# One transformer layer on one core: wider weight blocks in the second part of the first feed-forward input, and a new spread of the adaptive-norm rows

## The chip, the core and the metric

The kernel runs on one core of one Trainium2 chip, in one launch. The metric is the device time of the execution in microseconds. The time before is the median of 3 runs.

## What is computed

One layer with two feed-forward blocks around a token mixer. Every block is preceded by a modulated layer norm and followed by a gated residual and a second layer norm. The nine vectors of shift, scale and gate come from one condition vector `c`, through a matrix `w_ada` of 2048 x 18432:

```
ada = (jax.nn.silu(c) @ w_ada + b_ada)[:, None, :]
sh1, sc1, g1, sh2, sc2, g2, sh3, sc3, g3 = jnp.split(ada, N_ADA, axis=-1)
h = _swiglu(_modulate(x, sh1, sc1), ffn1_w_in, ffn1_w_out)
x = _layernorm(ALPHA * x + 0.5 * (1 + g1) * h, ln1_g, ln1_b)
h = _token_mixer(_modulate(x, sh2, sc2), w_in, ..., w_out)
x = _layernorm(ALPHA * x + (1 + g2) * h, ln2_g, ln2_b)
h = _swiglu(_modulate(x, sh3, sc3), ffn2_w_in, ffn2_w_out)
x = _layernorm(ALPHA * x + 0.5 * (1 + g3) * h, ln3_g, ln3_b)
```

`_swiglu` is `(silu(gate) * up) @ w_out`, where `gate` and `up` are the two halves of `h @ w_in`. There are 256 tokens, the model width is 2048, the feed-forward width 5632. All data is 32-bit floating point. The token mixer holds eight attention heads with a forget gate and four mLSTM heads.

## The kernel before

**Products.** Each weight block of 1 MB is loaded from memory by the SyncE queue (SP) into one of three `raw` buffers, and split into a high part (cast on ScalarE, line 155) and a low part (subtraction on VectorE, line 156), in two halves of 128 x 1024 elements. There are six buffers for each part, three blocks' worth. TensorE multiplies in three passes, high x high, high x low, low x high (`mm3`, lines 420 to 422).

**Stages, in order.** (1) The first four condition units and the first part of the first feed-forward input, `first_in`, names `s`: weight blocks of 512 inputs x 512 columns. (2) The second part of that input, `ffn_in`, names `f1i`: column pairs 12 to 21 of 256 columns each, gate and up. One step is one block of 1024 inputs x 256 columns. (3) The first output projection, `out_proj` with tag `f1`, names `f1o`: column groups of 1024, 512 and 512; a step ("unit") is 1 MB, so there are 22, 11 and 11 of them. The products of the last four units are kept for the end, where a layer norm (`boundary`) follows without a pause. (4) The mixer, steps of 1 MB each: output gate (`mo`), values (`fv`, `mv`), mLSTM queries and keys (`m`), attention queries and keys (`fb`, `fbk`, `fa`, `fak`), its output projection (`mxo`). `form_a_four` there takes its weights in blocks of 512 inputs x 512 columns. Between the products run the heads' short chains, written as generators that each step advances. (5) A second boundary, and the second feed-forward block (`gu`, `fh`, `fs`, `f2i`, `f2o`).

**The ada rows.** The product with `w_ada` is not done on TensorE. A unit of 1024 columns is built from 16 rows of 128 x 1024 elements. A row is one load of 512 KB (`ar`, line 189, on SP) into one of two `araw` buffers, and one multiply-add of 128 x 1024 on VectorE into an accumulator (`ada_acc`, lines 168 and 170). After the 16th row a tail of five small steps sums over the partitions (split, a TensorE product `bc`, and more VectorE work, lines 176 to 217).

**What sets their order.** `AdaQueue` holds 14 such units. After each weight step the program calls `pump(rate)`: the rate is added to what is owed, one tail step is made if a tail is open, and whole rows that are owed are issued. Each row is put behind the newest low part (`pinned`). A unit that uses the common accumulator can't begin while the tail of another such unit is open; what is owed meanwhile is issued afterwards. Units carry a stage number: seven may start in stage 0, four more after the first boundary, three after the second. `need(n)` finishes n units at once, where their result is used: 2 units before the first output projection, 6 at the first boundary, 10 late in the mixer's projection, then 11, 12 and 14. The rates (line 797) are `R_F` 1.25 in the end of the first part, `R_IN` 1.2 in `f1i`, `R_OUT` 1 in `f1o`, `R_MX` 1.42 in the mixer, `R_A` 1.05 and `R_B` 0.6 in the second block. In the last column group of an output projection the last four units issue no rows.

A step's loads, casts and multiply-adds run ahead of TensorE by what the buffers allow. VectorE takes its instructions in the order in which they were placed: a multiply-add whose row hasn't landed holds up what stands behind it.

The column loop of the second part, before, with its two cases; the first feed-forward takes the first of them:

```
for j in range(j0, DFF // 256):
    if values is None:
        ps = [mm_tile(f"gu_{tag}{j}_{f}") for f in range(2)]
        for gu in range(2):
            one(j, gu, [p[:, gu * T:(gu + 1) * T] for p in ps])
```

Of the kernel before, what the change touches and what calls it, by code (L numbers as in the profile page):

```python
# [14 lines left out]
P = 128  # L15
# [17 lines left out]
def layer_kernel(  # L33
# [408 lines left out]

    def ffn_in(w, xT, hT, j0, tag, npump, values=None):
        def one(j, gu, outs):
            last = gu and j == DFF // 256 - 1
            cols_form_a(w, gu * DFF + j * 256, outs, xT, f"{tag}i{j}_{gu}", (lambda: None) if last else npump)

        def both(dst, ps):
# [3 lines left out]
        for j in range(j0, DFF // 256):  # L452
            if values is None:
                ps = [mm_tile(f"gu_{tag}{j}_{f}") for f in range(2)]
                for gu in range(2):
                    one(j, gu, [p[:, gu * T:(gu + 1) * T] for p in ps])
                for f in range(2):
                    h = halves(hT[:, 2 * j + f, :])
                    S.activation(h, unwoven(ps[f][:, :T]), AF.Silu)
                    pin["h"] = V.tensor_tensor(out=h, in0=h, in1=unwoven(ps[f][:, T:]), op=ALU.mult).ins  # L460
                continue
            for gu in range(2):
                ps = [mm_tile(f"gu_{tag}{j}_{gu}{f}") for f in range(2)]
                one(j, gu, ps)
                for f in range(2):
                    h = halves(hT[:, 2 * j + f, :])
                    if gu:
                        u = halves(values.tile([P, T], F32, tag="u", bufs=2, name=f"u_{tag}{j}_{f}"))
                        both(u, ps[f])
                        pin["h"] = V.tensor_tensor(out=h, in0=h, in1=u, op=ALU.mult).ins  # L470
                    else:
                        both(h, ps[f])
                        S.activation(h, h, AF.Silu)
        for _ in range(2):
            npump()
# [3 lines left out]
    def out_proj(w, rows, nk, tag, npump, finish, before=None, turned=False, spare=None, fine=None):  # L479
# [12 lines left out]
        for width in (1024, 512, 512):  # L492
# [56 lines left out]
            for i, u in enumerate(us):  # L549
# [246 lines left out]

    R_F, R_IN, R_OUT, R_MX, R_A, R_B = 1.25, 1.2, 1, 1.42, 1.05, .6
    NP = 2
# [258 lines left out]
    first_hi_places("1")  # L1057
    ffn_in(W1, xT, hT, NS, "f1", at(R_IN))
    xp.release()
# [658 lines left out]
```

## Time and profile before

| what | value |
|---|---|
| median of 3 runs | 1876.1 us (1875.28 to 1876.51) |
| profiled execution, its own time | 1878.46 us |
| span of its trace | 1876.8 us |
| TensorE busy | 1829.0 us, 97% of the span |
| VectorE busy | 1465.0 us, 78% |
| ScalarE busy | 911.8 us, 49% |
| memory traffic | 510.74 MB, mean 272 GB/s |
| ada row loads | 230 on SP and 45 on GpSimd, 512 KB each |

PE is TensorE's multiplying, PEld its loading of weights, DVE is VectorE, ACT ScalarE, POOL GpSimd, SP SyncE. A row of a group reads: line, engine, operation, output and inputs with shapes, count, busy time in us and mean in ns, then idle time just before and what ended it. In rows by stretch of time, "DMA share" is the mean busy share of the 16 DMA engines, which can come out a little over 1, and PEclk is the clock that TensorE was granted.

### The profile page before, as it was taken

What the parts mean: (1) busy time and instruction counts of PE and PEld (TensorE: products, weight loads), DVE (VectorE), ACT (ScalarE), POOL (GpSimd) and SP (SyncE); (2) the same over time, 40 slices, a digit from 0 to 9 for tenths busy, and PEclk for the clock granted to TensorE, in tenths of its full rate; (3) what the DMA queues carried; (4) which work ended last, traced back from release to release, by engine and by line L of the source; (5) the groups of instructions that cost most, each with busy time, mean ns of one, the idle gap of its engine ahead of it and who ended that gap; (6) DMA issues with size and microseconds to landing.
All of it is one profiled execution on the core that took longest, in us unless ns stands there. A gap on an engine that the chain in (4) does not pass through costs nothing.

```text
span 1876.8 us, 29775 instructions
## 1 busy us (share of the span) xinstructions
PE 1829.0 (97%) x11881; PEld 1673.8 (89%) x11881; DVE 1465.0 (78%) x1883; ACT 911.8 (49%) x1320; POOL 62.2 (3%) x92
## 2 busy tenths in 40 slices
PE   7999999999999999999989999999999999999997
PEld 5999999999998888699989887888999999988887
DVE  6888989778788886878879788988977766574655
ACT  3554363443454433845556545565444454554441
POOL 1211200000000000100000000000000000000000
PEclk9999999999999999999999999999999999999999
DMA  9988978999998898489978894998878776666664
GB/s 365 383 279 294 333 232 274 313 312 325 296 315 305 309 329 296 136 301 331 316 254 307 303 314 142 307 305 265 271 253 265 260 241 193 201 202 204 205 204 146
DMA packets 283906, 510.74 MB, mean 272 GB/s; under 512 B 10834, under 2 KB 134386, under 8 KB 282744
## 3 DMA queue, kind: packets, MB, share of 16 engines
q1 hardware_dynamic: 275656, 477.90, 75.0%
q0 software_dynamic: 8112, 30.95, 4.8%
q8 instruction: 93, 1.52, 0.3%
q14 instruction: 45, 0.37, 0.1%
HBM read 506.71 MB, written 2.10 MB: 271 GB/s over the span
## 4 chain that ended last, share of the span: by engine, by line
PE 38%; DMA 10%; DVE 8%; issue 2%; ACT 2%; POOL 0%; DVEq 0%; ACTq 0%; SPq 0%; POOLq 0%
PE gu_f L425 9%; DMA ar<-in_w_ada_dram 7%; PE gu_f L426 4%; PE o_f L421 4%; PE o_f L420 4%; PE o_f L422 4%; PE fs L425 3%; DMA raw_fh<-in_ffn_w_in_dram 2%; DVE acc L170 2%; PE fs L426 1%; DVE gate L170 1%; PE fh L425 1%; PE b_mv L421 1%; PE b_mv L420 1%; PE b_mv L422 1%
## 5 line engine op out<-in xcount | busy, mean ns | idle before, releaser
L170 DVE SCALAR_TENSOR_TENSOR acc<-ar,csil,acc 128x1024 f32<-128x1024 f32 (+1 forms) x167 | 211.7, 1269 | 74.3 <-DMA ar<-in_w_ada_dram 73.7
L425 PE MATMUL gu_f<-x_f,hi_f2i 128*128 128x512 f32 x768 | 251.8, 382 | 0.0
L422 PE MATMUL s<-x_f,lo_s 128*128 128x256 f32 x768 | 211.9, 276 | 0.8 <-DVE lo_s L156 0.7
L420 PE MATMUL s<-x_f,hi_s 128*128 128x256 f32 x768 | 212.2, 277 | 0.2 <-ACT x_f L336 0.2
L421 PE MATMUL s<-x_f,hi_s 128*128 128x256 f32 x768 | 212.0, 276 | 0.0
L426 PE MATMUL gu_f<-x_f,lo_f2i 128*128 128x256 f32 x768 | 209.3, 273 | 0.0
L422 PE MATMUL gu_f<-x_f,lo_f1i 128*128 128x256 f32 x640 | 176.4, 276 | 1.4 <-DVE lo_f1i L156 1.3
L421 PE MATMUL gu_f<-x_f,hi_f1i 128*128 128x256 f32 x640 | 176.0, 275 | 0.0
L420 PE MATMUL gu_f<-x_f,hi_f1i 128*128 128x256 f32 x640 | 176.0, 275 | 0.0
L156 DVE TENSOR_TENSOR lo_f2o<-raw_f2o,hi_f2o 128x1024 fp32r<-128x1024 f32 x86 | 105.2, 1225 | 86.9 <-ACT hi_f2o L155 86.8
L156 DVE TENSOR_TENSOR lo_f2i<-raw_f2i,hi_f2i 128x1024 fp32r<-128x1024 f32 x96 | 117.5, 1224 | 65.7 <-ACT hi_f2i L155 64.8
L425 PEld LDWEIGHTS gu_f<-x_f,hi_f2i 128*128 128x128 f32 x768 | 145.1, 189 | 20.3
L155 ACT CAST hi_s<-raw_s 128x1024 fp32r<-128x1024 f32 x96 | 99.5, 1051 | 128.7 <-PE s L421 77.0
L422 PEld LDWEIGHTS s<-x_f,lo_s 128*128 128x128 f32 x768 | 147.9, 193 | 1.2 <-DVE lo_s L156 1.2
L421 PEld LDWEIGHTS s<-x_f,hi_s 128*128 128x128 f32 x768 | 147.9, 193 | 0.4 <-DVE x_f L339 0.4
L420 PEld LDWEIGHTS s<-x_f,hi_s 128*128 128x128 f32 x768 | 147.8, 193 | 0.3 <-ACT x_f L336 0.3
L426 PEld LDWEIGHTS gu_f<-x_f,lo_f2i 128*128 128x128 f32 x768 | 147.4, 192 | 0.2
L155 ACT CAST hi_f2o<-raw_f2o 128x1024 fp32r<-128x1024 f32 x86 | 90.0, 1047 | 115.7 <-PE o_f L422 107.5
L155 ACT CAST hi_f2i<-raw_f2i 128x1024 fp32r<-128x1024 f32 x96 | 100.4, 1045 | 91.3 <-PE gu_f L425 65.3
L155 ACT CAST hi_f1o<-raw_f1o 128x1024 fp32r<-128x1024 f32 x86 | 88.5, 1047 | 113.7 <-DMA raw_f1o<-in_ffn_w_out_dram 55.0
L170 DVE SCALAR_TENSOR_TENSOR gate<-ar,csil,gate 128x1024 f32<-128x1024 f32 (+1 forms) x94 | 117.6, 1252 | 29.0 <-DMA ar<-in_w_ada_dram 28.9
L155 ACT CAST hi_f1i<-raw_f1i 128x1024 fp32r<-128x1024 f32 x80 | 81.3, 1049 | 111.6 <-DMA raw_f1i<-in_ffn_w_in_dram 80.2
(449 smaller groups left out, 5095.4 us busy)
## 6 DMA issues: line engine op xcount, KB each, us to landing
ar<-in_w_ada_dram SPq DMA_DIRECT2D x230, 512.0 KB, 5.5
raw_f2i<-in_ffn_w_in_dram SPq DMA_DIRECT2D x48, 1024.0 KB, 5.2
raw_s<-in_ffn_w_in_dram SPq DMA_DIRECT2D x47, 1024.0 KB, 7.6
raw_f1o<-in_ffn_w_out_dram SPq DMA_DIRECT2D x44, 1024.0 KB, 7.3
raw_f2o<-in_ffn_w_out_dram SPq DMA_DIRECT2D x44, 1024.0 KB, 5.2
raw_f1i<-in_ffn_w_in_dram SPq DMA_DIRECT2D x40, 1024.0 KB, 7.8
ar<-in_w_ada_dram POOLq DMA_DIRECT2D x45, 512.0 KB, 6.4
raw_mxo<-in_w_out_dram SPq DMA_DIRECT2D x16, 1024.0 KB, 7.7
```

What stands on the lines that cost most here:

```text
L155: S.copy(hi, src)
L156: return V.tensor_tensor(out=lo, in0=src, in1=hi.bitcast(F32), op=ALU.subtract)
L170: V.scalar_tensor_tensor(out=acc, in0=raw, scalar=csil[:, k:k + 1], in1=acc, op0=ALU.mult, op1=ALU.add)
L420: PE.matmul(o, ah, bh, start=start, stop=False)
L421: PE.matmul(o, ah, bl, start=False, stop=False)
L422: PE.matmul(o, al, bh, start=False, stop=stop)
L425: PE.matmul(o, ah, x.rearrange("p s (a n) -> p s n a", a=2), start=start, stop=False)
L426: PE.matmul(o[:, T:], al, woven(x[:, 0]), start=False, stop=stop)
```

## The change

The second part of the first feed-forward input gets a loop of its own, `ffn_in_512`. A step now loads 512 inputs x 512 columns (rows of 2 KB in memory where they had 1 KB); four steps make up the gate half of 512 columns and four the up half. Two PSUM tiles hold four feature blocks, two in each. The gate's SiLU is taken after its four steps, the product with up after the other four. `ffn_in` loses the case that only the first feed-forward used. Three numbers of the ada queue change: `R_IN` 1.2 to 1.4, `R_MX` 1.42 to 1.15, and in the last column group of the first output projection two units instead of four issue no rows.

```diff
+    def ffn_in_512(w, xT, hT, q0, tag, npump):
+        xhi, xlo, _ = xT
+        for q in range(q0, DFF // 512):
+            for gu in range(2):
+                ps = [mm_tile(f"gu_{tag}{q}_{gu}{i}") for i in range(2)]
+                for u in range(4):
+                    c0 = gu * DFF + q * 512
+                    for k4, hi, lo in load_w(w[u * 512:(u + 1) * 512, c0:c0 + 512], 4, 512, f"{tag}i{q}_{gu}{u}"):
+                        k = 4 * u + k4
+                        for f in range(4):
+                            fs = slice(f * P, (f + 1) * P)
+                            mm3(ps[f // 2][:, f % 2 * T:(f % 2 + 1) * T], hi[:, fs], lo[:, fs], xhi[:, k, :], xlo[:, k, :],
+                                k + f % 2 == 0, k + f % 2 == KD)
+                    if not (gu and q == DFF // 512 - 1 and u > 1):
+                        npump()
+                for f in range(4):
+                    h, p = halves(hT[:, 4 * q + f, :]), unwoven(ps[f // 2][:, f % 2 * T:(f % 2 + 1) * T])
+                    if gu:
+                        pin["h"] = V.tensor_tensor(out=h, in0=h, in1=p, op=ALU.mult).ins
+                    else:
+                        S.activation(h, p, AF.Silu)
         for _ in range(2):
             npump()
...
-                if not lastg or i < nu - 4:
+                if not lastg or i < nu - (2 if tag == "f1" else 4):
                     npump()
...
-    R_F, R_IN, R_OUT, R_MX, R_A, R_B = 1.25, 1.2, 1, 1.42, 1.05, .6
+    R_F, R_IN, R_OUT, R_MX, R_A, R_B = 1.25, 1.4, 1, 1.15, 1.05, .6
...
-    ffn_in(W1, xT, hT, NS, "f1", at(R_IN))
+    ffn_in_512(W1, xT, hT, NS // 2, "f1", at(R_IN))
```

More of the change, by code (lines that the diff above doesn't have):

```diff
@@ L441, in cols_form_a, with ffn_in @@
             npump()
[L443 to L446, printed above, removed]
+    def ffn_in(w, xT, hT, j0, tag, npump, values):
         def both(dst, ps):
@@ L452, in ffn_in @@
         for j in range(j0, DFF // 256):
[L453 to L461, printed above, removed]
             for gu in range(2):
                 ps = [mm_tile(f"gu_{tag}{j}_{gu}{f}") for f in range(2)]
-                one(j, gu, ps)
+                last = gu and j == DFF // 256 - 1
+                cols_form_a(w, gu * DFF + j * 256, ps, xT, f"{tag}i{j}_{gu}", (lambda: None) if last else npump)
                 for f in range(2):
```

2 lines of the change are left out of this document (added).

## The prediction

> **What bounds the kernel now.** I read the page first, then the busy time by stage, then what TensorE waited for in each stage, then VectorE's order at the longest of those waits.
>
> ```profile
> span 1876.8 us, 29775 instructions
> PE 1829.0 (97%) x11881; PEld 1673.8 (89%) x11881; DVE 1465.0 (78%) x1883; ACT 911.8 (49%) x1320; POOL 62.2 (3%) x92
> ```
>
> TensorE is busy 97% of the span. The change removes no matmul, so it can only touch the 47.8 us in which TensorE is idle. The stretches below are, in order, the second part of the first input, the first output projection, the mixer, and two of the second block.
>
> ```profile
> core 0: us, PE busy (x) PEld busy (x) DVE busy (x) ACT busy (x) POOL busy (x), PEclk, DMA share, GB/s
> 307.00:521.00 214.00, 212.59 (x1884) 211.31 (x1883) 164.37 (x168) 89.10 (x107) 1.08 (x2) 1.00 0.94 308
> 521.00:742.00 221.00, 221.00 (x1048) 193.48 (x1048) 184.75 (x189) 99.63 (x111) 1.06 (x2) 1.00 0.90 317
> 795.00:1147.00 352.00, 338.07 (x2330) 316.14 (x2329) 294.87 (x426) 187.48 (x339) 7.22 (x11) 1.00 0.88 304
> 1176.00:1275.00 99.00, 96.18 (x573) 87.61 (x572) 84.59 (x111) 57.92 (x98) 0.58 (x1) 1.00 0.97 317
> 1275.00:1640.00 365.00, 363.24 (x2182) 331.75 (x2182) 272.32 (x357) 181.20 (x255) 1.61 (x3) 1.00 0.74 242
> ```
>
> Idle time of TensorE: 1.4 us in the second part, none in the output projection, 13.9 us in the mixer, 2.8 and 1.8 us in the second block. So the stage that gets the new blocks has almost nothing to give, and the stage that loses rows has 13.9 us. These are TensorE's waits, all of the mixer's first, then all of the second part's:
>
> ```profile
> PE sps L1428 <- DVE dm L1434: 5.0, 1, 5.0
> PE o_mx L422 <- DVE ylo L156: 2.9, 1, 2.9
> PE o_mx L420 <- ACT yF L1251: 2.1, 1, 2.1
> PE pr_fb L422 <- DVE lo_fb L156: 1.5, 1, 1.5
> PE b_fv L421 <- DVE lo_fv L156: 1.0, 1, 1.0
> PE b_mv L421 <- DVE lo_mv L156: 0.8, 1, 0.8
> PE bc L183 <- DVE alo L156: 0.4, 1, 0.4
> PE o_mx L420 <- DVE res L540: 0.3, 1, 0.3
> ...
> PE gu_f L422 <- DVE lo_f1i L156: 1.3, 2, 1.1
> ```
>
> No DMA stands in that list: TensorE waits for VectorE, seven times out of eight in the mixer. What VectorE was doing at the longest wait, the 5.0 us for `dm`:
>
> ```profile
> 946.19 1.28 DVE L170 SCALAR_TENSOR_TENSOR acc<-ar,csil,acc 128x1024 f32<-128x1024 f32 x1
> 952.17 1.28 DVE L170 SCALAR_TENSOR_TENSOR acc<-ar,csil,acc 128x1024 f32<-128x1024 f32 x1 [4.71 <-DMA ar<-in_w_ada_dram]
> 953.38 0.68 DVE L200 TENSOR_TENSOR dg<-bc,ident 128x512 f32<-128x512 f32 x1
> 954.10 0.69 DVE L202 TENSOR_REDUCE scsh<-dg 128x4 f32<-128x512 f32 x1
> ...
> 954.90 0.49 DVE L1433 TENSOR_TENSOR dm<-dm,trir 128x128 f32<-128x128 f32 x2
> 955.30 0.42 DVE L1434 TENSOR_TENSOR dm<-sps,dm 128x256 f32<-128x256 f32 x1
> ```
>
> VectorE stood for 4.71 us before a row that had not landed, then made that row's multiply-add and a unit's tail, and only then the 0.9 us that TensorE needed. The wait of `b_fv` has the same form on the chain of waits, a row, its multiply-add, a row:
>
> ```profile
> 813.92 1.30 DVE acc L170
> 815.23 6.81 DMA ar<-in_w_ada_dram
> 822.13 1.28 DVE acc L170
> ```
>
> The groups of VectorE say how much of this there is, for the mixer (first two), the second part (next two) and the output projection:
>
> ```profile
> L170 DVE SCALAR_TENSOR_TENSOR acc<-ar,csil,acc 128x1024 f32<-128x1024 f32 x45 | 57.7, 1282 | 29.4 <-DMA ar<-in_w_ada_dram 29.4
> L170 DVE SCALAR_TENSOR_TENSOR gate<-ar,csil,gate 128x1024 f32<-128x1024 f32 x30 | 38.4, 1279 | 11.3 <-DMA ar<-in_w_ada_dram 11.2
> ...
> L170 DVE SCALAR_TENSOR_TENSOR acc<-ar,csil,acc 128x1024 f32<-128x1024 f32 x28 | 35.9, 1282 | 18.9 <-DMA ar<-in_w_ada_dram 18.9
> L170 DVE SCALAR_TENSOR_TENSOR gate<-ar,csil,gate 128x1024 f32<-128x1024 f32 x15 | 19.2, 1282 | 10.8 <-DMA ar<-in_w_ada_dram 10.7
> ...
> L170 DVE SCALAR_TENSOR_TENSOR acc<-ar,csil,acc 128x1024 f32<-128x1024 f32 x39 | 50.0, 1281 | 18.9 <-DMA ar<-in_w_ada_dram 18.4
> ```
>
> VectorE stands 40.6 us for rows in the mixer, 29.6 in the second part, 18.4 in the projection. In the last two nearly all of it falls into the lead that casts have over TensorE; in the mixer the heads' short chains have no lead.
>
> **Where the rows go.** I ran the queue's rules by hand. Steps: the second part has 40 before (10 pairs x 2 x 2) and after (5 x 2 x 4), each of 1 MB, with 40 calls of the pump either way. At 1.2 and 1.4 that asks for 48 and 56 rows. But a unit on the common accumulator waits for five tail steps, and after the change this pause falls on the stage's last steps, so 48 and 53 rows are issued there. The projection has 40 calls before and 42 after, and takes 37 rows before, 45 after (those left over included). The mixer has 57 calls: 80 rows before, 65 after. The second block takes 48 and 50, 18 of them before its two halves meet either way. All 14 units are then done as before; the six that the first boundary needs are complete at both, and after the change the seventh has 13 of its 16 rows. So 15 rows leave the mixer: 5 go to the second part, 8 to the projection, 2 to the second block.
>
> **Mixer.** One row is 0.524 MB. The mixer's 304 GB/s at a share of 0.88 is 345 GB/s for a full share, so 15 rows are 15 x 1.52 = 22.8 us of DMA time, and 15 x 1.28 = 19.2 us of VectorE. Its DMA share falls from 0.88 to 0.82, VectorE's from 84% to 78%. The two row buffers turn more slowly: a row every 352/80 = 4.4 us becomes one every 5.4 us. What that is worth, wait by wait. `b_fv` and `b_mv`, 1.8 us, come straight from late rows: I take off 1.2. The group around the heads, `pr_fb`, `bc` and `sps`, is 6.9 us, and it costs the clock as well:
>
> ```profile
> 940.00:960.00 20.00, 13.92 (x100) 13.14 (x101) 15.23 (x23) 9.67 (x20) 0.55 (x1) 0.91 0.69 229
> ```
>
> A mean of 0.91 over 20 us is 3.6 us at half speed, or 1.8 us of work lost: 8.7 us together. After the change five rows instead of six belong to the four steps of `fb`, and the tail that stood in the way falls into the steps of `m`: I take off 6.0. The waits in the output projection of the mixer, 5.3 us, stand behind rows in part (a copy on ScalarE, a low part): I take off 2.5. Against this, the tails now fall beside other chains, which I price at 1.5 us, between 0 and one wait of the longest kind, 6.8 with its clock. Mixer: -9.7 + 1.5 = -8.2, with ends of -15.7 (all waits and the clock) and +5.
>
> **Second part.** Matmuls, casts, low parts and evacuations are the same in number and size, in another order; the mixer's `form_a_four` has that order and TensorE's pace there is that of the second part:
>
> ```profile
> L421 PE MATMUL gu_f<-x_f,hi_f1i 128*128 128x256 f32 x640 | 176.0, 275 | 0.0
> L421 PE MATMUL pr_m<-x_mx,hi_m 128*128 128x256 f32 x128 | 35.2, 275 | 0.0
> ```
>
> Both take 275 ns, so the order costs nothing. PSUM turns over at two tiles per four steps as before. The loads: stages with blocks 256 columns wide move 308/0.94 = 328 and 317/0.97 = 327 GB/s for a full share, the mixer with 512 columns 345. The stage now moves 308 x 214 = 65.9 MB; with 5 rows more 68.5. At 345 that takes 198.6 us of the 214, a share of 0.93; at 328 it is 208.9, a share of 0.98. I take 345, since the mixer's blocks have the shape of the new ones. While the queue isn't paused, a step asks for 1.049 + 1.4 x 0.524 = 1.78 MB, 5.17 us at 345, where it now is 1.68 MB, 5.12 us at 328; a step lasts 214/40 = 5.35 us. So the extra rows are paid for by the wider blocks, with nothing over. VectorE gets 5 x 1.28 = 6.4 us more and has 50 idle. I add 0.5 us to the 1.3 us of waits, with ends of -1.3 and +6.
>
> By the Trainium skill (DMA: Bandwidth & Descriptors, Specifications) a transfer of 512 B or more already runs at line rate, so blocks with 1 KB rows would move as fast as those with 2 KB. By that rule the stage would stand at the share of 0.98, which is the second rival below; the 328 against 345 GB/s of this trace speaks against the rule, though the stages differ in more than the row's length.
>
> **First output projection and boundary.** 8 rows more are 4.2 MB; at 317/0.90 = 352 GB/s that is 11.9 us of DMA, share 0.95, and 10.2 us of VectorE, 88%. TensorE has no wait there now; I add 0.5, up to +4. Two more units issue rows just ahead of the boundary, and rows that a tail used to hold back now run through the last group. VectorE has room there:
>
> ```profile
> 721.83 1.29 DVE L393 TENSOR_TENSOR dlo<-raw_f1o,dhi 128x512 fp32r<-128x512 f32 x2 [4.29 <-ACT dhi L390]
> ...
> 731.86 2.36 DVE L156 TENSOR_TENSOR lo_f1o<-raw_f1o,hi_f1o 128x1024 fp32r<-128x1024 f32 x2 [2.98 <-ACT hi_f1o L155]
> ```
>
> It idles 4.3 and 3.0 us for casts, which themselves wait for TensorE to free buffers; about five rows fit. If one lands late ahead of a low part, TensorE's last products wait: +0.5, up to +3. The second block's two rows fall into a stage at a share of 0.74: nothing, with 1.3 us each if that cover failed.
>
> **Sum.** -8.2 + 0.5 + 0.5 + 0.5 = -6.7 us. The profiled execution took 1878.46 us, 1.7 over its span and 2.4 over the median of the runs. It would come to 1871.8, the median to 1876.1 - 6.7 = 1869.4.
>
> **Rivals.** First, waits that depend on place, not on number: `dm`, `yF` and `ylo` end chains of several engines, and whichever row stands ahead of them holds them up. For it: only two of the eight waits are of blocks' low parts behind a late row alone. Against: VectorE's largest idle group is rows. Then the mixer gives 1.2 and takes 1.5, the first block takes 1.5: 1878, no change.
>
> Second, the wider blocks save no DMA time. The second part stands at 0.98 and a step at 1.4 rows needs 1.78/0.328 = 5.43 us, more than its 5.35. Over unpaused runs of twelve steps that is 1 us each time, and where the lead is gone TensorE waits as it did for 1.1 us: some 4 us over the stage instead of 0.5. Total -8.2 + 4 + 0.5 + 0.5 = -3.2: 1872.9. This is what the rule from the Trainium skill (DMA: Bandwidth & Descriptors, Specifications) would lead to.
>
> Third, slower: the rows' two buffers become the limit in the second part. At 1.4 a buffer must turn in 2 x 5.35/1.4 = 7.6 us; a row takes this to land:
>
> ```profile
> raw_f1i<-in_ffn_w_in_dram SPq DMA_DIRECT2D x37, 1024.0 KB, 7.7
> ar<-in_w_ada_dram SPq DMA_DIRECT2D x46, 512.0 KB, 5.0
> ```
>
> 5.0 us, 1.3 for its multiply-add, and the weight load ahead of it on the queue takes 7.7. A row issue that waits for its buffer holds the next weight load behind it on SP, VectorE stands before the row, and the low parts come late. It decides once the casts' lead is shorter than the 4.7 us wait seen above. Priced by the mixer, 13.9 us for 80 rows, 53 rows cost 9.2 us and 1.8 of clock, less today's 1.3: +9.7; the mixer saves by the same price 15 x 0.17 = 2.6. Total +7: 1883.
>
> **How the numbers follow.** Forecast 0.55, waits by place 0.19, no DMA saving 0.13, slower 0.13. The range of 1862 to 1877 goes from 14 us of the mixer's 15.7 saved to just over no change, which leaves out the third rival and part of the first. A difference of 0.2%, 3.8 us, is about what a measurement of this kernel can tell from no change. Faster by more: nearly all of the forecast and under half of the second rival, 0.60. Within: 0.25. Slower: 0.15, the third rival and the first with a long new wait.
>
> **What would show it.** Right: 65 rows in the mixer, its idle time near 5 us, no wait of `sps` for `dm` of 5 us and a clock of 1.00 there; DMA share of the second part 0.93 to 0.95 at over 320 GB/s, and TensorE idle under 3 us in it; none in the projection beyond 1 us. Wrong: the mixer's idle time above 10 us with fewer rows, or over 5 us of waits for low parts in the second part or at the first boundary.

## The result and the profile after

The median went from 1875.69 us (1871.53 to 1876.51, 4 runs) to 1892.53 us (1889.75 to 1895.59, 4 runs): a ratio of 1.0095, 95% interval 1.0071 to 1.0118. The change makes the kernel slower by some 17 us. The profiled execution took 1889.75 us, 11.3 more than that of before; it is the fastest of its four, while the one of before lies 2.8 us over its median.

From the page of after, the span and the engines:

```profile
span 1888.0 us, 29767 instructions
PE 1836.3 (97%) x11881; PEld 1681.0 (89%) x11881; DVE 1468.8 (78%) x1883; ACT 914.5 (48%) x1320; POOL 62.0 (3%) x92
```

The counts of instructions on the compute engines are those of before. The same work took longer, so the place has to be found by stage. The table gives the time from the first product of a stage to the first of the next, from the two timelines of TensorE.

| stage | before | after | difference | forecast |
|---|---|---|---|---|
| first part of the input (`s`) | 272.3 | 275.3 | +2.9 | 0 |
| second part (`f1i`) | 219.6 | 231.1 | +11.4 | +0.5 |
| first output projection and boundary (`f1o`) | 233.0 | 250.6 | +17.6 | +1.0 |
| mixer | 400.0 | 383.5 | -16.5 | -8.2 |
| second boundary | 26.1 | 26.1 | 0.0 | 0 |
| start of the second block (`fh`, `gf`) | 103.0 | 98.7 | -4.4 | 0 |
| the rest of it (`fs`, `f2i`, `f2o`) | 577.4 | 577.4 | 0.0 | 0 |

So the mixer gained twice what was forecast, and the two stages that took the rows lost nearly twice what the mixer gained. A single profile scatters: `s`, whose code is the same in both, lies between 269.0 and 275.7 us in 18 further profiles, so its 2.9 us say nothing, and what the other stages scatter by is weighed behind the first experiments. Busy time by stretch, after: the second part, the first output projection, the mixer. PEclk, DMA share and GB/s are the last three columns.

```profile
310.00:541.00 231.00, 220.91 (x1934) 219.04 (x1933) 176.16 (x177) 89.65 (x109) 1.08 (x2) 0.99 0.89 307
541.00:792.00 251.00, 238.45 (x1077) 206.04 (x1076) 199.86 (x223) 105.98 (x122) 3.13 (x4) 0.97 0.84 292
827.00:1163.00 336.00, 335.26 (x2333) 315.47 (x2332) 280.91 (x413) 188.97 (x340) 7.06 (x11) 1.00 0.86 296
```

TensorE is idle 0.7 us in the mixer, where it was 13.9. In the second part it is idle 10.1 us (1.4 before), in the projection with its boundary 12.6 us. The same stretch of before, from its first product to the mixer's:

```profile
526.60:759.60 233.00, 232.01 (x1074) 201.83 (x1072) 190.89 (x214) 103.62 (x122) 3.14 (x4) 1.00 0.85 298
```

There TensorE was idle 1.0 us. Over the two stages the DMA share went down, from 0.94 to 0.89 and from 0.85 to 0.84: on the mean, memory is not what they wait for. What TensorE waited for in the three stretches, in the same order; a row says engine, line, releaser, us in total, times, longest:

```profile
PE bc L183 <- DVE alo L156: 4.9, 1, 4.9
PE gu_f L422 <- DVE lo_f1i L156: 2.7, 3, 1.1
PE gu_f L420 <- ACT hi_f1i L155: 2.5, 2, 1.4
...
PE o_f L420 <- ACT hi_f1o L155: 4.7, 1, 4.7
PE o_f L420 <- DVE hT L483: 3.4, 1, 3.4
PE o_f L420 <- DVE res L552: 3.0, 1, 3.0
...
PE lps L1300 <- DVE dn L1457: 0.7, 1, 0.7
```

Four waits of 3.0 to 4.9 us make up 16.0 of the 22.7 us that are idle in the first two stretches. Each stands at a hand-over: the tail of a gate's unit (`alo`), the last products of `hT` between the two stages, the evacuation of PSUM at a change of column group (`res`), and the start of the last four units (`hi_f1o`). At the last of them the weights were late. ScalarE's cast had waited 7.09 us for its block, while the DMA engines were full; a mean over the stage hides this:

```profile
756.00:771.00 15.00, 10.79 (x50) 9.11 (x49) 8.53 (x9) 4.35 (x5) 1.06 (x2) 0.95 1.03 393
...
770.41 1.99 ACT L155 CAST hi_f1o<-raw_f1o 128x1024 fp32r<-128x1024 f32 x2 [7.09 <-DMA raw_f1o<-in_ffn_w_out_dram]
```

The four waits cost the clock as well. The stretches around and behind them:

```profile
426.00:446.00 20.00, 15.20 (x117) 15.11 (x118) 15.73 (x17) 7.13 (x11) 0.54 (x1) 0.83 0.86 297
546.00:556.00 10.00, 9.31 (x35) 7.85 (x36) 8.89 (x14) 7.41 (x14) 0.00 (x0) 0.83 0.76 279
663.00:676.00 13.00, 10.00 (x39) 8.38 (x39) 13.00 (x16) 3.45 (x4) 0.00 (x0) 0.87 0.83 275
767.00:787.00 20.00, 15.03 (x59) 12.54 (x60) 13.09 (x20) 6.33 (x8) 1.53 (x1) 0.83 0.84 302
```

The clock in these stretches is either 1.00 or 0.50 in nearly every single microsecond, so a mean of 0.83 over 20 us is 6.8 us at half speed, over 10 us 3.4: together 20.4 us. Not all of it costs work. Around the waits for `alo` and `hi_f1o` the clock falls while TensorE still waits, 2.2 and 2.7 us after it stopped, so that only about 4.1 and 4.3 of the 6.8 us fall on products. That leaves some 15.2 us at half speed, or 7.6 us of work: 2.1 in the second part and 5.5 in the projection. Idle time and clock give 10.1 - 1.4 + 2.1 = 10.8 us for the second part (measured 11.4) and 12.6 - 1.0 + 5.5 = 17.1 for the projection (measured 17.6): the loss is nearly accounted for. The Trainium skill (TensorE: Matmul & The Clock Gate, Part 1) says that the clock falls to half after an idle window of about 3.4 us and comes back after as long a busy one. The trace has dips of 3.4 us and of twice that, but the clock fell after shorter idle times, 2.2 and 2.7 us, and after a wait of only 3.0 us.

What VectorE did at the first of these waits (start, duration, instruction, idle before it):

```profile
421.45 2.35 DVE L156 TENSOR_TENSOR lo_f1i<-raw_f1i,hi_f1i 128x1024 fp32r<-128x1024 f32 x2
426.73 1.28 DVE L170 SCALAR_TENSOR_TENSOR acc<-ar,csil,acc 128x1024 f32<-128x1024 f32 x1 [2.92 <-DMA ar<-in_w_ada_dram]
427.93 0.69 DVE L215 SCALAR_TENSOR_TENSOR gate<-bc,gate 128x512 f32<-128x512 f32 x1
428.53 1.28 DVE L170 SCALAR_TENSOR_TENSOR acc<-ar,csil,acc 128x1024 f32<-128x1024 f32 x1
429.72 0.42 DVE L217 TENSOR_SCALAR gate<-gate 128x512 f32<-128x512 f32 x1
430.06 0.69 DVE L156 TENSOR_TENSOR alo<-gate,ahi 128x512 fp32r<-128x512 f32 x1
```

It stands 2.92 us for a row, sums it, takes a step of a tail, sums another row, and only then makes the 0.69 us of `alo` that TensorE has been waiting for since 425.86. That is the form of the wait for `dm` that the mixer had before. At the change of column group it is the same, with the rows between the evacuations:

```profile
661.20 1.28 DVE L170 SCALAR_TENSOR_TENSOR acc<-ar,csil,acc 128x1024 f32<-128x1024 f32 x1 [2.14 <-DMA ar<-in_w_ada_dram]
662.40 1.22 DVE L156 TENSOR_TENSOR lo_f1o<-raw_f1o,hi_f1o 128x1024 fp32r<-128x1024 f32 x1
663.53 0.69 DVE L550 TENSOR_TENSOR o_f<-o_f,gate 128x512 f32<-128x512 f32 x1
664.14 1.27 DVE L170 SCALAR_TENSOR_TENSOR acc<-ar,csil,acc 128x1024 f32<-128x1024 f32 x1
665.33 0.68 DVE L552 SCALAR_TENSOR_TENSOR res<-res,o_f 128x512 f32<-128x512 f32 x1
```

TensorE waits from 663.16 for `res`. So the kind of wait that left the mixer, a row ahead of a short step, is found again in the two stages ahead of it. The experiments ask what part of the change brought them, and what about the rows makes them.

### The profile page after: what moved, and what is told of

It reads as the page before. It is cut to its first block, busy times and chain, and to the rows that moved or that the text cites. A ratio compares the mean times of both kernels' runs of the same rounds, so it can differ in the third digit from the quotient of the medians.

```text
span 1888.0 us, 29767 instructions
## 1 busy us (share of the span) xinstructions
PE 1836.3 (97%) x11881; PEld 1681.0 (89%) x11881; DVE 1468.8 (78%) x1883; ACT 914.5 (48%) x1320; POOL 62.0 (3%) x92
## 4 chain that ended last, share of the span: by engine, by line
PE 54%; DVE 1%; ACT 1%; issue 1%; DMA 1%; POOL 0%; DVEq 0%; ACTq 0%; POOLq 0%
PE gu_f L425 9%; PE gu_f L426 4%; PE o_f L420 4%; PE o_f L421 4%; PE o_f L422 4%; PE fh L425 3%; PE fs L425 3%; PE fh L426 1%; PE fs L426 1%; PE o_mx L422 1%; PE o_mx L421 1%; PE o_mx L420 1%; PE b_mv L420 1%; PE b_fv L420 1%; PE b_mv L421 1%; PE b_fv L421 1%
## 5 line engine op out<-in xcount | busy, mean ns | idle before, releaser
L420 PE MATMUL o_f<-hi_f1o,hi 128*128 128x512 f32 x344 | 132.7, 386 | 11.1 <-ACT hi_f1o L155 4.7
```

The lines of the kernel that those rows point to most:

```text
L420: PE.matmul(o, ah, bh, start=start, stop=False)
```

## The experiments

Each kernel was timed against the kernel before on the same chip. Numbers by stage are from one profile each; the ratios are of medians.

**The new loop alone.** Before, with `ffn_in_512` in place of `ffn_in` and nothing else.

```diff
-    ffn_in(W1, xT, hT, NS, "f1", at(R_IN))
+    ffn_in_512(W1, xT, hT, NS // 2, "f1", at(R_IN))
```

> Only the loop with blocks of 512 columns; rates and the four silent units as before. Theory R (the rows that were moved into the first feed-forward make VectorE and the weight loads late there): no change against before, 1873 to 1878 us, TensorE's waits in the second part near 1 us, in the first output projection none, the mixer's waits of 10 us and more stay. Theory B (the new loop itself, four evacuations at once and four products with up at its end, costs the time): 1885 to 1895 us, with the waits of about 5 us in the second part and 3 us at the start of the projection.

Measured 1878.51 us, ratio 1.002 (0.9989 to 1.005); `f1i` 220.9, mixer 396.1. No difference can be seen: by the interval the loop alone costs at most 0.5% and gains at most 0.1%.

**The numbers alone.** Before, with its old loop:

```diff
-                if not lastg or i < nu - 4:
+                if not lastg or i < nu - (2 if tag == "f1" else 4):
-    R_F, R_IN, R_OUT, R_MX, R_A, R_B = 1.25, 1.2, 1, 1.42, 1.05, .6
+    R_F, R_IN, R_OUT, R_MX, R_A, R_B = 1.25, 1.4, 1, 1.15, 1.05, .6
```

> The old loop with 256 columns; the three changed numbers of the ada queue. Theory R: as slow as the changed kernel or a little slower, since 1 KB rows leave less DMA time: 1888 to 1900 us, waits of 10 us or more in the projection, the mixer nearly free of waits. Theory B: the mixer's gain of 16 us without the loop's cost: 1858 to 1866 us.

Measured 1888.93 us, ratio 1.0097 (1.0068 to 1.0125): the whole loss. `f1i` 228.4, `f1o` 255.2, mixer 384.4, and the same four waits in the list of what TensorE waited for:

```profile
PE o_f L420 <- DVE hT L460: 6.4, 1, 6.4
PE bc L183 <- DVE alo L156: 5.6, 1, 5.6
PE o_f L420 <- ACT hi_f1o L155: 5.3, 1, 5.3
PE o_f L420 <- DVE res L540: 3.4, 1, 3.4
```

Where the rows go is the cause, and the wider blocks do not pay for them.

**Four silent units.** In the changed kernel:

```diff
-                if not lastg or i < nu - (2 if tag == "f1" else 4):
+                if not lastg or i < nu - 4:
```

> The changed kernel, but the last four units of the first output projection issue no rows, as before. If the rows in the last group are the cost (theory E): the 4.7 us wait for a high part at the end of the projection and its slow clock are gone, 8 us faster than the changed kernel, 1882 to 1885 us. Theory R, which puts the cost on all the rows that were moved: 3 to 8 us faster, the waits of 3 us at the start of the projection and at its change of column group stay. Theory B: no change, 1890 to 1894 us.

Measured 1896.34 us, ratio 1.0129 (1.0105 to 1.0153). The wait at the start of the last units shrank from 4.7 to 1.2 us for `hi_f1o` and 0.8 for a low part, but the one for `hT` was 7.7 and `f1o` 251.3. Two of the theories had expected a faster kernel; it did not come. The two added units make the wait for `hi_f1o`, but they are not the cause of the loss.

**The mixer's number alone.** In the kernel before:

```diff
-    R_F, R_IN, R_OUT, R_MX, R_A, R_B = 1.25, 1.2, 1, 1.42, 1.05, .6
+    R_F, R_IN, R_OUT, R_MX, R_A, R_B = 1.25, 1.2, 1, 1.15, 1.05, .6
```

> Only the mixer's rate goes from 1.42 to 1.15. All units are then behind: by hand, five rows and a tail are forced late in the mixer's output projection, nine rows and a tail before the second block's second half. Theory R: the mixer up to its projection gains 10 to 14 us as in the changed kernel, the forced rows cost about 9 x 1.5 + 5 x 1.5 = 21 us of DMA time in two places of which half shows; 1870 to 1885 us. If the mixer's gain does not come from fewer rows but from their new places, its waits stay above 10 us.

Measured 1891.28 us, ratio 1.0099 (1.0062 to 1.0136). The mixer fell to 388.7, so its gain needs only fewer rows there. But rows that are not made early have to be made when `need` asks for them, and TensorE then stands for the chain of the tails:

```profile
PE bc L183 <- ACT ahi L155: 19.7, 4, 8.9
```

The stage `fs` took 116.3 us instead of 95.6. The mixer's gain can't be had by leaving rows out of it; they need a place.

These runs also give the scatter by stage. `f1i` and `f1o` have the rows of before in three profiles (before, the loop alone, the mixer's number alone): 219.6, 220.9 and 218.5 us, and 233.0, 238.6 and 241.3. The last two of `f1o` have a wait of 3.6 and 4.7 us at the boundary, for the cast of a tail (`ahi`), that the profile of before happens not to have. With the rows of the change, or two fewer (99 to 101 in the two stages by the traces, where they were 87), in three profiles (after, the numbers alone, four silent units): 231.1, 228.4 and 228.9, and 250.6, 255.2 and 251.3. By the means, 219.7 to 229.5 and 237.6 to 252.4, the rows cost 9.8 and 14.8 us, 24.6 together. The mixer takes 400.0 and 396.1 with `R_MX` 1.42, and 383.5, 384.4, 387.6 and 388.7 with 1.15: a gain of some 12 us by the means. That leaves 12.6 of the 17 us between the medians; the rest is not to be placed in single profiles.

**At most two rows a step.** The changed kernel with the loop of `pump` cut off after two rows, so that what a tail held back comes out in smaller bursts.

```diff
-            while self.owed >= 1:
+            for _ in range(2):
+                if self.owed < 1:
+                    break
```

> The changed kernel, but a step issues at most two rows; what a pause leaves owed is spread over later steps. As many rows as in the changed kernel come before the boundary. If the bursts of 5 to 8 rows after a pause make the waits at the start of the first output projection, at its change of column group and at its end (theory P, place): those three waits fall from 11 us together to under 4 us and the stage from 251 to about 238 us, 1875 to 1882 us. If the number of rows does it (theory N): within 4 us of the changed kernel, 1888 to 1896 us.

Measured 1892.06 us, ratio 1.009 (1.0062 to 1.0117). `f1i` was 232.9 and `f1o` 251.0, now with 6.2 us before `res`, 4.0 before `hi_f1o` and 3.7 before `alo`. Bursts alone are not the cause.

**Half the move.** The changed kernel with four silent units, as above, and other numbers, by which the two stages take 7 rows more than before (94 in the trace):

```diff
-    R_F, R_IN, R_OUT, R_MX, R_A, R_B = 1.25, 1.4, 1, 1.15, 1.05, .6
+    R_F, R_IN, R_OUT, R_MX, R_A, R_B = 1.25, 1.3, 1, 1.25, 1.05, .6
```

> Wide blocks, rate 1.3 in the second part, 1.25 in the mixer, four silent units: 7 rows more than before ahead of the first boundary where the change has 13. Theory N: half the cost and half the gain, second part and projection together about 467 us (453 before, 482 after), mixer up to the second block's first products about 391 (400 and 385), 1879 to 1886 us. Theory P: anything between 1872 and 1893, by where the pauses fall, and the two sums not near the middle.

Measured 1878.89 us, ratio 1.0029 (0.9999 to 1.0059). `f1i` and `f1o` together 469.1, by the means above 457.3 with the rows of before and 481.9 with those of the change; mixer 390.2. About half of the rows give about half of the loss and over half of the gain. This one profile shows no threshold between.

**Small loads, and small sums.** Two kernels that leave part of the computation out, so that the row's two costs come apart. In the first, 15 of 16 rows of seven early units are loaded only in 32 columns, and VectorE makes a multiply-add of the full size that doesn't read the row; most of those units' columns are therefore not summed. In the second the rows are loaded in full and only 32 columns of them are summed.

```diff
+    early = ["2_0", "2_1", "3_0", "3_1", "3_2", "3_3", "6_0"]
...
-            SP.dma_start(raw, src[k * P:(k + 1) * P])
-            ada_acc(acc, raw, k)
+            if tag in early and k:
+                few = slice(0, 32)
+                SP.dma_start(raw[..., few], src[k * P:(k + 1) * P, ..., few])
+                ada_acc(acc[..., few], raw[..., few], k)
+                V.scalar_tensor_tensor(out=acc, in0=acc, scalar=csil[:, k:k + 1], in1=acc, op0=ALU.mult, op1=ALU.add)
...
-            ada_acc(acc, raw, k)
+            few = slice(0, 32 if tag in early and k else None)
+            ada_acc(acc[..., few], raw[..., few], k)
```

> The changed kernel with the loads of 15 of the 16 rows in each of the first seven queue units cut to a sixteenth of their bytes or less, and the full multiply-add replaced by one of the same size on the accumulator that does not read the row; the values of these ada units are left out. VectorE's work stays, the DMA's goes. If late rows are what holds VectorE (theory L, landing): the second part falls from 231 to 214 to 217 us, the projection from 251 to 222 to 226 us. If VectorE's own time is the limit (theory V): both stay over 225 and 240 us.

> The changed kernel with full loads, but the multiply-adds of 15 of the 16 rows in each of the first seven queue units take only 32 of the columns; most of these ada values are left out. The DMA's work stays, about 100 x 1.2 = 120 us of VectorE's goes. Theory L: the waits stay in kind, since an instruction that waits for a late row holds VectorE as long whatever its size; second part over 222 us, projection over 238 us. Theory V: 214 to 217 and 222 to 226 us.

Each of the two took the whole loss away: 1853.55 us with small loads and 1858.53 with small sums, one run each. Each theory expected one of them to stay slow, so neither holds as it was stated. Busy time in the second part and the projection, small loads:

```profile
307.00:525.00 218.00, 217.56 (x1924) 216.56 (x1924) 192.85 (x235) 96.76 (x115) 1.08 (x2) 1.00 0.69 221
525.00:758.00 233.00, 231.45 (x1068) 201.24 (x1067) 202.65 (x260) 103.82 (x122) 3.81 (x5) 1.00 0.65 209
```

and small sums:

```profile
311.00:528.00 217.00, 217.00 (x1924) 216.25 (x1923) 126.11 (x179) 92.85 (x112) 1.07 (x2) 1.00 0.93 329
528.00:760.00 232.00, 231.00 (x1068) 201.40 (x1068) 154.66 (x218) 103.46 (x121) 3.13 (x4) 1.00 0.86 305
```

With small loads VectorE is busy 192.9 us of 218, more than in the changed kernel, and TensorE doesn't wait: VectorE's work alone is no bound at 88%. With small sums the memory moves 329 GB/s, more than the 307 of the changed kernel, and TensorE doesn't wait: the loads alone are no bound either. With small sums VectorE even stands longer for rows. Its waits in the second part of the changed kernel,

```profile
DVE lo_f1i L156 <- ACT hi_f1i L155: 26.1, 13, 5.3
DVE acc L170 <- DMA ar<-in_w_ada_dram: 22.0, 17, 3.5
DVE gate L170 <- DMA ar<-in_w_ada_dram: 5.0, 5, 1.5
```

and with small sums:

```profile
DVE acc L170 <- DMA ar<-in_w_ada_dram: 42.0, 26, 4.2
...
DVE gate L170 <- DMA ar<-in_w_ada_dram: 18.6, 12, 3.2
```

Here VectorE's standing for rows cost TensorE nothing, with little VectorE work behind it. The loss takes the late row and the full sums together.

**The rows on GpSimd's queue.** Weight loads wait behind row loads on SP. In `ada_rows`, first of the changed kernel, then of the one before:

```diff
-            SP.dma_start(raw, src[k * P:(k + 1) * P])
+            G_.dma_start(raw, src[k * P:(k + 1) * P])
```

> The changed kernel with the ada rows issued on GpSimd's queue, so that a row that waits for its buffer no longer stands ahead of the next weight load on SP. If the shared queue is what makes the added rows dear (theory Q, the third rival of the prediction): second part and projection together fall from 482 to under 465 us, the whole to 1865 to 1880 us. If it is VectorE's time together with the DMA's (theory N): both stay within 5 us of 482, 1886 to 1898 us.

> The kernel before with the rows on GpSimd's queue. Theory Q: the mixer's waits, which come from late rows behind weight loads, shrink by half, 1862 to 1870 us. Theory N: no more than 4 us either way, 1870 to 1880 us.

The changed kernel took 1898.7 us, ratio 1.011 (1.0093 to 1.0127): no relief, with 9.8 us before `res` and 5.5 before `hT`. But VectorE then stood 45.6 and 28.5 us for rows in the two stages, where it stood 27.0 and 14.0: on the other queue the rows come later, and this price may hide a relief. Whether sharing SP's queue costs anything is not shown. The kernel before took 1926.37 us, ratio 1.0273 (1.0241 to 1.0305), its mixer 426.6 instead of 400.0, with several low parts late there:

```profile
PE pr_m L422 <- DVE lo_m L156: 4.4, 3, 2.7
PE b_fv L421 <- DVE lo_fv L156: 3.7, 3, 2.1
PE b_mv L421 <- DVE lo_mv L156: 3.6, 1, 3.6
```

I had not expected this. VectorE's standing for rows in the mixer rose from 44.0 to 71.3 us there, and in the changed kernel, with fewer rows in its mixer, from 14.4 to 27.1. That fits a larger loss, but no run separates why the same edit costs 2.7% in one kernel and next to nothing in the other.

**Less VectorE work in the projection.** The changed kernel with the low part of the projection's left-hand side made on GpSimd instead of VectorE, 44 subtractions.

```diff
-            V.tensor_tensor(out=lo, in0=rows, in1=hi.bitcast(F32), op=ALU.subtract)
+            G_.tensor_tensor(out=lo, in0=rows, in1=hi.bitcast(F32), op=ALU.subtract)
```

> The changed kernel with the low part of the projections' inner rows (128 x 512, 18 of them in the first projection at 0.69 us) taken by GpSimd instead of VectorE: 12 us of VectorE less in the projection, as much as 10 rows' multiply-adds. Theory V2 (in the projection VectorE's share of 80% with what it stands for leaves no room, so its time is what the 8 more rows cost): the projection falls from 251 to 238 to 244 us, the second part stays at 231, 1878 to 1886 us. If VectorE's time is not the price there: 1888 to 1896 us. If GpSimd is too slow for it, new waits for `lo` and over 1896 us.

Measured 1894.31 us, ratio 1.01 (1.0085 to 1.0115); `f1o` 260.9, worse. The groups of this run show where the saving went:

```profile
L1114 POOL TENSOR_TENSOR lo<-hT,hi 128x512 fp32r<-128x512 f32 x44 | 83.6, 1901 | 401.4 <-ACT hi L1112 398.5
...
L156 DVE TENSOR_TENSOR lo_f1o<-raw_f1o,hi_f1o 128x1024 fp32r<-128x1024 f32 x86 | 110.4, 1303 | 33.0 <-ACT hi_f1o L155 32.8
```

The subtraction takes 1901 ns on GpSimd, and VectorE's own low parts take 1303 ns, where the changed kernel's take 1221. VectorE was busy some 204 us in this stage, where it was 200 in the changed kernel. The experiment didn't take the load off, so it says little about the cause.

**More rows in the projection, none more in the second part.** The changed kernel with four silent units and the low part on GpSimd, as above, and other numbers:

```diff
-    R_F, R_IN, R_OUT, R_MX, R_A, R_B = 1.25, 1.4, 1, 1.15, 1.05, .6
+    R_F, R_IN, R_OUT, R_MX, R_A, R_B = 1.25, 1.2, 1.3, 1.15, 1.05, .6
```

> Wide blocks, rate 1.2 in the second part as before, 1.3 in the first projection, 1.15 in the mixer, four silent units, low part on GpSimd: 111 rows before the boundary where the change has 109, all of the moved ones in the projection. If the rows are cheaper where VectorE has been relieved: second part 220, projection 238 to 246, mixer 384, 1863 to 1876 us, the only one of these that would beat the kernel before. Theory N, a price of about 2 us for a row wherever it goes: projection 255 to 262 us, 1880 to 1892 us.

Measured 1887.98 us, ratio 1.006 (1.0037 to 1.0084): `f1i` 221.1, `f1o` 261.5 with 8.9 us before `res`, mixer 383.6. The second part is back at its time of before, and the projection holds the loss; how much of it is GpSimd's, as in the run above, this run can't tell.

**No rows around the hand-overs.** The changed kernel, with at most two rows a step, and no rows issued in the two steps at either side of a change of column group, in the projection's first two steps, and in the two closing calls of `ffn_in_512`. What is owed is made later.

```diff
+        def hold(self, n):
+            self.owed += n
+            self.end_step()
...
-            npump()
+            ada.hold(R_IN)
...
+                if tag == "f1" and (i < 2 or not lastg and i >= nu - 2):
+                    ada.hold(R_OUT)
+                elif not lastg or i < nu - (2 if tag == "f1" else 4):
```

> The changed kernel with at most two rows a step, and no rows in the two steps on either side of each change of column group in the first projection nor at its start; what is owed is made up between. If the place of the rows on VectorE's queue is the cause (theory H, hand-over): the waits for `hT` and `res` at these points go from 3 to 8 us to under 1 us, the projection from 251 to 238 us, 1876 to 1884 us. If the number is (theory N): the waits move to other places (low parts, the end), projection over 246 us, 1888 to 1896 us.

Measured 1879.66 us, ratio 1.0034 (1.0012 to 1.0056). Against 1.0095 that is 0.6%, some 11 us. What TensorE waited for in the projection:

```profile
PE tp L361 <- DVE n L355: 3.3, 1, 3.3
PE o_f L426 <- DVE hT L489: 3.3, 1, 3.3
PE o_f L427 <- DVE lo_f1o L156: 1.5, 2, 0.8
PE o_f L426 <- ACT hi_f1o L155: 1.4, 1, 1.4
```

The wait for `res` is gone and that for `hi_f1o` is 1.4 instead of 4.7; that for `hT` stayed, and the boundary has a wait of 3.3 us for the layer norm (`n`) that is 0.6 in the changed kernel. `f1o` is 244.4, `f1i` 229.4, the mixer keeps its 384.4. With the two kernels below that have the same edit, `f1o` has a mean of 244.5 (244.4, 248.9, 240.1) against 252.4, and `f1i` of 228.1 against 229.5. So 9 of the 24.6 us are a matter of place, nearly all of them in the projection; the rows, as many as in the changed kernel (101 in the two stages by the trace), still cost the other 15 elsewhere.

**A longer gate tail, and both.** One more `yield` ahead of the product `bc` of a gate's tail, so that `alo` has a step more; then this together with the edit above.

```diff
             yield
+            yield
             bc = ada_sum(parts, f"{v}_{j}_{i}")
```

> The changed kernel with one step more between a gate tail's split and its TensorE product. Theory H: the wait of 4.9 us for the low part in the second part and its 3.4 us of clock go, second part from 231 to 223 to 225 us, the rest as it was, 1883 to 1888 us. Theory N: the wait moves, second part over 228 us, 1888 to 1896 us.

> Both edits. Theory H: second part 224, projection 238, 1870 to 1878 us. Theory N: within 5 us of the changed kernel, 1887 to 1897 us.

The longer tail alone: 1891.72 us, ratio 1.0088 (1.006 to 1.0116). The wait for `alo` went, and its time came back at low parts of `f1i` (233.0) and at `hT` (8.2 us). Both: 1882.2, ratio 1.0039 (1.0018 to 1.006), no better than the first edit alone. Taking one wait away by its place moved the time on.

**Half the move with both edits.**

> Both edits on the version with half the rows moved (rates 1.3 and 1.25, four silent units; 227 and 242 us in the two stages, 390 in the mixer). Theory H: 222 and 236 us, mixer 386 to 390, 1862 to 1870 us, faster than the kernel before. Theory N: as without the edits, 1875 to 1882 us.

Measured 1890.62 us, ratio 1.009 (1.0062 to 1.0118). `f1o` is 234.4, the time of before, and the second part 225.4. But by the trace the two stages hold 87 rows, as many as before, so this is not a relief by place: the held rows were not caught up, and `fs` took 113.0 us instead of 95.6, as when only the mixer's number was changed. What was gained was paid back where `need` forces rows.

**Rows in halves.** Nothing is left out here: each row is loaded as two halves and summed by two multiply-adds, so that the first half's sum falls into the standing for the second. First in the changed kernel, then in the one without rows at the hand-overs.

```diff
-            SP.dma_start(raw, src[k * P:(k + 1) * P])
-            ada_acc(acc, raw, k)
+            pair = len(acc.shape) == 3
+            for i in range(2):
+                h = (slice(None), i) if pair else (slice(None), slice(i * 512, (i + 1) * 512))
+                SP.dma_start(raw[h], src[(slice(k * P, (k + 1) * P),) + h[1:]])
+            for i in range(2):
+                h = (slice(None), i) if pair else (slice(None), slice(i * 512, (i + 1) * 512))
+                ada_acc(acc[h], raw[h], k)
```

> The changed kernel, with each row loaded in two halves of 128 x 512 and summed by two multiply-adds of 128 x 512 (about 0.69 us each, as the trace has for 128 x 512 elsewhere, against 1.28 for one whole); the same two row buffers, all results kept. If what costs is VectorE making a whole sum after a row that landed late (standing plus 1.28 us ahead of the next low part or evacuation), the first half's sum now falls into the standing: about 0.6 us less for each of the some 34 late rows of the second part and the first projection, 20 us of VectorE, so a half or more of the 29 us that the two stages lost comes back, about 1880, ratio near 1.004. If instead VectorE's total is what counts, each row costs 0.1 us more and nothing comes back: 1893 to 1898, ratio 1.010 to 1.013, with the waits for alo, hT, res and hi_f1o as they were.

> The kernel that issues no rows around the change of column group, the start and the end of the first projection and at most two a step, with the rows in halves as well. If late rows' sums cost and half sums relieve them, this adds to the hand-over edit: 1879.7 less some 5 to 10 us, 1870 to 1875, ratio 0.997 to 1.000, the first that would reach the kernel before. If the total of VectorE counts, it stays at 1880 or a little over, ratio 1.003 to 1.007.

Measured 1891.76 us, ratio 1.0109 (1.0088 to 1.013), and 1882.39 us, ratio 1.0052 (1.0033 to 1.007): nothing gained in either. The group of the halves, in the second part of the first of them:

```profile
L170 DVE SCALAR_TENSOR_TENSOR acc<-ar,csil,acc 128x512 f32<-128x512 f32 x72 | 50.8, 746 | 14.4 <-DMA ar<-in_w_ada_dram 14.1
```

VectorE stood less before these rows (14.4 us; 22.0 in the changed kernel), and for all rows of the stage 23.1 us where it was 27.0. But two halves keep it busy 1.41 us, 50.8 us for 36 rows, where a whole row took 1.28, and it is busy 183.8 us in the stage where it was 176.2. What the halves save in standing they cost in work, so this does not tell whether the length of one sum behind a late row matters.

No version that computes the whole layer beat the kernel before.

## Why the prediction was wrong, step by step

**What bounds the kernel.** Right as far as it went: TensorE waits for VectorE, and in the mixer it waits because rows stand in front of short chains. The rows were counted nearly right: the trace of after has 65 multiply-adds of rows in the mixer (80 before), and 55 and 46 in the stretches of the other two stages, by hand 53 and 45. That is 14 more than before in these two stages, by hand 13.

**Mixer.** The mechanism was right, the size was not: -16.5 us between the two profiles, -12 by the means, for -8.2. Nearly all waits went, not two thirds of them; TensorE's idle time fell from 13.9 to 0.7 us and the clock stood at 1.00. The 1.5 us for tails falling beside other chains were not needed. The start of the second block gained 4.4 us, which no step had; with the numbers alone it took 101.3 us, so most of this may be scatter.

**Second part.** This is the step that failed: "So the extra rows are paid for by the wider blocks, with nothing over. VectorE gets 5 x 1.28 = 6.4 us more and has 50 idle." The stage lost 11.4 us, 9.8 by the means, for a forecast of 0.5, beyond its bound of 6. The first half of the step was about a resource that didn't decide: the wide blocks alone changed nothing measurable (ratio 1.002, 0.9989 to 1.005). The second half took VectorE's idle time for room. It was none. VectorE's waits in that stretch of the kernel before:

```profile
DVE acc L170 <- DMA ar<-in_w_ada_dram: 18.9, 11, 3.9
DVE lo_f1i L156 <- ACT hi_f1i L155: 15.8, 7, 4.4
DVE gate L170 <- DMA ar<-in_w_ada_dram: 10.7, 6, 4.9
DVE acc L168 <- DMA ar<-in_w_ada_dram: 3.1, 1, 3.1
```

Of the 50 us it stood 32.7 for rows and 15.8 for casts. While it stands for a row, VectorE makes nothing of what is placed behind it, as the order at `alo` shows. The added rows did not bring more standing: it was 27.0 us in this stage after. Nor do the sums alone fill the stage, since with small loads VectorE works 192.9 us there and TensorE doesn't wait. What the timelines show is a late row with its full sum ahead of a step that TensorE needs next. A sign that the prediction had named for being wrong is there, over 5 us of waits for low parts in the second part: 4.9 for `alo` and 2.7 for `lo_f1i`.

**Output projection and boundary.** The same failure, for 1.0 us forecast and 17.6 measured, 14.8 by the means, outside the bounds of 4 and 3. "TensorE has no wait there now" and "VectorE has room there" were read from means and from one place near the boundary. The stage has three more places, at `hT`, at the change of column group and at the last units, where TensorE has nothing queued but what VectorE or a cast hands over next. There a row or two ahead of the hand-over is a wait of 3 us and more, and each of these costs 1.7 to 2.1 us of work by the clock. The share of 0.95 for the DMA engines was a mean as well: ahead of the last units they were full, and with four silent units most of that wait was gone. Of the two casts that the prediction has waiting for TensorE, the first waited 4.47 us for its load. The prediction priced the clock in the mixer, where it goes away, and not where it could come.

**The second block's two rows.** Right: nothing was lost there.

**The rivals.** The third, slower by buffers and queue, came nearest in its result for the second part (+9.7 forecast, +11.4 measured) and named the right signs, VectorE standing before a row and the low parts late. The half of its mechanism that goes through SP's queue got no support from the rows on GpSimd's queue, and no refutation; the half that goes through the two row buffers fits the small loads and the small sums, both of which shorten a buffer's turn, but was not tested by itself: no run has a third row buffer. SP's own waits don't bear it out: in the second part its row loads stood 73.7 us for VectorE's earlier sums with the loop alone, where nothing was lost, and 70.3 with the numbers alone, where all of it was. This rival did not have the projection, where most of the loss is. The first rival, waits by place, was wrong for the mixer and holds for 8 of the 14.8 us lost in the projection. The second, no saving of DMA time, gave the right loop result for another reason. By the Trainium skill (DMA: Bandwidth & Descriptors, Specifications) blocks with 1 KB rows already run at line rate. The second part moved 307 GB/s at a share of 0.89, 345 for a full share, against 328 before, and with the loop alone 309 at 0.90, or 343, so the trace does not agree on the rate; but the time didn't depend on it.

**What stays open.** That the rows in these two stages are the cause is shown, as is that it takes their loads and their sums together, and that some 9 of 25 us go by the places around the projection's hand-overs. How the other 15 come about is not settled. They moved between `alo`, `hT` and the low parts of `f1i` when one of them was relieved, and grew with the number of rows; that it is the turn of the two row buffers, or the queue they share with the weights, is only argued.

## What to carry to other kernels

Idle time of an engine that works in order is not room by itself: ask first what it stands for, and what an added instruction would stand for too. Before work is moved into a stage in which TensorE never waits, list the hand-overs in it, where TensorE has nothing queued beyond one engine's next result, and price each at its wait and the clock behind it. A mean share of memory over a stage says nothing of such a place. Work with a due time that is held back from all such places comes out at its due time, at 17 to 21 us here.

## What the runs showed of the hardware

GpSimd takes 1901 ns for a subtraction of 128 x 512 that takes VectorE 690, and while it works the same VectorE instruction of 128 x 1024 goes from 1221 to 1303 ns. A multiply-add of 128 x 512 takes 746 ns and one of 128 x 1024 1281. Two in a row overlap, so a pair keeps VectorE busy 1.41 us: halving costs 10%. Loading 224 rows more through GpSimd's queue cost the kernel before 2.7%, with no more bytes, and the changed kernel nothing that can be told from its own loss. A small load is not a quick one behind large ones on the same queue: rows of 16 to 32 KB took 2.8 to 4.9 us to land in the second part and the projection, whole rows of 512 KB 5.1 and 5.5 in the changed kernel. TensorE's clock was at half for 3.4 or 6.8 us around waits of 3.0 to 4.9 us, and fell as early as 2.2 us into one.
